# Decoder layer on one core: the first two output tiles projected together, the third as filling, and w_out's splits called later

## The chip, the core and the metric

The kernel runs on 1 core of one Trainium2 chip. The metric is the device time of one execution in microseconds (us). TensorE (PE; its weight loads PEld) does the matrix products into PSUM banks, VectorE (DVE) and ScalarE (ACT) the elementwise work, GpSimd (POOL) a little of it, and the SP queue issues the DMAs.

## The reference

One layer of a hybrid decoder, for a prompt of 2048 tokens and a sample of 8 x 8 tokens, all in float32, D_MODEL 1024:

```python
h = rms_norm(x, g_mix_pre)
proj = h @ w_in                      # q, k, v | gq, gk, gv, gr, glr
attn = swa_banded(q, k, v, sinks)    # window 128, 8 query heads on 2 key heads
log_a = log_sigmoid(glr @ w_gk2 + b_gk) / 16
o, s_new = gla_chunked(gq, gk, gv, log_a, s0)       # 4 heads, dk 64, dv 128
gla_out = rms_norm(o, g_gla) * silu(gr)
x = x + rms_norm(concat(attn, gla_out) @ w_out, g_mix_post)
u = relu(rms_norm(x, g_ffn_pre) @ w_up)
x = x + rms_norm((u * u) @ w_down, g_ffn_post)
```

The outputs are x for prompt and sample, the last 128 keys and values, and the states of the gated linear attention (GLA).

## The kernel before, in words

Tokens are cut into 17 tiles: 0 to 15 are 128 prompt tokens each, 16 (NB) is the sample. For accuracy each matrix product is made as three products of high and low parts: a tensor is "split" by a ScalarE copy that rounds (the high part) and a VectorE subtraction (the low part); `split_copy`, lines 225 and 226, is that pair.

The stages follow one another: window attention with its projections; GLA over tiles 0 to 15; the output projection with its residual and second norm; the up and down projections of the MLP. The change lies at the end of GLA and the beginning of the output projection.

GLA. `gla(i, gp, og)` is a generator that works off one tile: transposes of queries and keys (qk), decay sums (es, kd), the output gate (sg), the diagonal (pr, dg), seven levels of decayed products (`level_sums`, `leveled`: dec, XK, XQ), products of keys and queries for two levels at a time (gm), masked copies of these into AT (line 1008), the state (ds, S), the output o, its norm (ojunk, ors, og) and the output's transposes (ogT). `decayed(i)` makes the next tile's decays (pg, z, zt, tT) between the gm groups. Nearly all of this is VectorE and ScalarE work with small matmuls. To keep TensorE busy meanwhile, the generator yields numbers, and the loop that drives it then issues so many matmuls of `fill = products()`:

```python
for n, free in chain.from_iterable(parts):
    deque(islice(fill, n // 2), 0)
    for _ in range(free):
        next(side, None)
    deque(islice(fill, n - n // 2), 0)
```

For each tile the slots are 38, 14, 9, 9, 9 and 13 (`G_FILL`, `G_GM`); tile 0 has 24 instead of 38 and 20 for its own decays; the last tile has another 44 ahead of ogT. `side` is the sample's GLA.

`products()` first yields GLA's own input projection, gproj, chunk by chunk (`G_ORDER` = 3, 0, 1, 2, of 24 matmuls a tile each, the sample 16): 1408 matmuls in all. In the last tile of it, tile 15, the weights of a chunk are used for the last time, and their places take w_out: `load_wo(ks, c)` loads the pieces k of w_out (128 rows each) for the place of chunk c, over four staging places in turn (`raws[k % 4]`: two gx buffers, s0, gp_s), and splits them into `wo[k]`; its calls are spread, one for each 8 matmuls. `load_mix(i)` loads a tile's mixed features (attention and GLA outputs, transposed, from DRAM) into a place of chunk 3's weights, of which there are two in turn, and splits them. After gproj, `products()` yields the output projections (`out_projecting`) of the first two tiles of `B_ORDER` = 0, 4, 1, 5, 2, 6, 3, 7, 16, 8, 12, ..., 15: for each tile two banks, one after the other, of 8 steps k x 3 products. The lists `early` and `mixes` carry banks and features on.

What `fill` has left is issued after tile 15 (`deque(fill, 0)`). Then the loop over `B_ORDER[2:-1]` issues `out_proj(i)` for each next tile (line 1250), and `residual` for the tile two before it: squares of the banks (line 1394) and their sum (1395), the scaling by the norm (1401, which frees the banks), the addition of x (1405), the second norm (1407, 1410), transposes (xnT, 1426) and copies of these. PSUM has 8 banks: kinds a, b and c with two, d and e with one; `next_bank(kinds, ...)` goes round a string of kinds.

The instructions of an engine run in the order that is fixed when the kernel is built. `te`, `ac` and `dv` (`InOrder`) keep the order of the code; for calls through `nc.` that order can differ from the code's, as the trace shows (the first splits of w_up, called in the loop eleven tiles later, stand at 789.56 us). In the trace most calls through `te`, `ac`, `dv` and `sy` have line 139.

Of the kernel before, what the change touches and what calls it, by code (L numbers as in the profile page):

```python
# [23 lines left out]
KT = D // P  # L24
T = 2048
NB = T // P
# [35 lines left out]
G_NEXT = (NB, *range(2, NB))  # L62
G_ORDER = (3, 0, 1, 2)
G_FILL, G_GM = (38, 14, 13), 9
S_WAIT = (2, 3, 6)
WO_PARTS = ((), (0, 1, 2), (3, 4, 5), (6, 7))
B_ORDER = (*(j + b for j in range(4) for b in (0, 4)), NB, *(j + b for j in range(4) for b in (8, 12)))
# [57 lines left out]
def f32(ap):  # L125
    return ap.bitcast(F32)
# [23 lines left out]
def hybrid_step_kernel(ctx: ExitStack, tc: tile.TileContext, I, O):  # L150
    nc = tc.nc
# [11 lines left out]
    def rows(i):  # L163
        return min(P, NTOK - i * P)
# [7 lines left out]
    te, ac, dv = (InOrder(tc, engine) for engine in (nc.tensor, nc.scalar, nc.vector))  # L172
# [5 lines left out]

        return ps.tile(shape, F32, tag=kind, name=name, bufs=1 if kind in "de" else 2)

    turns = {"aabb": 0, "cdce": 0}

    def next_bank(kinds, name):
        turns[kinds] += 1
        return bank([P, 512], kinds[(turns[kinds] - 1) % len(kinds)], name)
# [37 lines left out]
    def split_copy(hi, lo, src, vector=nc.vector):  # L223

        nc.scalar.activation(hi, src, AF.Copy)
        vector.tensor_tensor(lo, src, f32(hi), op=ALU.subtract)
# [432 lines left out]
    def run(products, n=None):  # L659
        deque(products if n is None else islice(products, n), 0)  # L660
# [118 lines left out]
    for i in range(NB):  # L779
# [17 lines left out]
        if i >= NB - 2:  # L797
            t = i - NB + 2
# [100 lines left out]
    def x_place(name, shape=(P, KT, P), kind=F32R):  # L899
        return [sp.tile(list(shape), kind, tag=f"gx{u}", name=f"gx{u}_{name}", bufs=2) for u in range(2)]  # L900
# [160 lines left out]
    def gla(i, gp, og=iter(())):  # L1061
# [20 lines left out]
        for l, b in enumerate(LEVELS):  # L1082
            level_sums(before, after, dec, l, b)
            leveled(XK if l else None, XQ, dec, qk, l, b, P)
        yield G_FILL[1], 2
        following = decayed(i + 1, gps[i + 1]) if i < NB - 1 else iter(())
        nc.scalar.activation(dec[:, :, NL, :], before, AF.Exp, scale=1.0 / 16)
        qd = next(qds)
# [131 lines left out]
            te.transpose(ob[:NS, h, :], s_oT[:, h, :], ident)  # L1220
        yield from finish_out(i, lambda h: ob[:NS, h, :], sg, NS, "b")

    def load_mix(i):
        n = rows(i)
        p_, c = gw[G_ORDER[0]][0], G_ORDER[0]
        m = p_.tile([P, 3, KT, P], F32R, tag=f"w{c}{(B_ORDER.index(i) + 1) % 2}", name=f"mt_{i}")
        ks = KT // 2 if i == NB - 1 else KT
        nc.sync.dma_start(f32(m[:, 0, :ks, :n]), mix_d[i][:, :ks])
        if i == NB:
            split_copy(m[:, 1, :, :NS], m[:, 1, :, NS:], f32(m[:, 0, :, :NS]))  # L1230
            return m[:, 1], None
        split_copy(m[:, 1, :ks, :n], m[:, 2, :ks, :n], f32(m[:, 0, :ks, :n]))
        parts = [[m[:, u, k, :n] for k in range(ks)] for u in (1, 2)]
        if i == NB - 1:
            for t, late in zip(parts, late_mix):
                t.extend(late[:, h, :] for h in range(4))
        return parts

    def out_projecting(te, i, banks):
        mh, ml = mixes.pop(i, None) or load_mix(i)  # L1240
        for c in range(2):
            p_ = next_bank("aabb", f"out_{i}_{c}")
            cc = slice(c * 512, (c + 1) * 512)
            for k in range(KT):
                if i == NB:
                    products = [(mh[:, k], w) for w in wo[k]]
                else:
                    products = (mh[k], wo[k][0]), (mh[k], wo[k][1]), (ml[k], wo[k][0])
                for u, (x, w) in enumerate(products):
                    te.matmul(p_, x, w[:, cc], start=k + u == 0, stop=k == KT - 1 and u == len(products) - 1)  # L1250
                    yield
            banks.append(p_)
# [7 lines left out]
    def load_wo(ks, c):  # L1260

        parts = [gw[c][0].tile([P, 3, D], F32R, tag=f"w{c}{u}", name=f"wo{u}_{c}") for u in range(2)]
        if len(ks) == 2:
            late_mix.extend(t[:, 2, :512].rearrange("p (h t) -> p h t", h=4) for t in parts)
        for n, k in enumerate(ks):
            wo[k] = [t[:, n, :] for t in parts]
            raw = raws[k % 4]
            if k < 4:
                for r in range(2):
                    e0 = r * 256 + k * HD  # L1270
                    nc.sync.dma_start(raw[r * HD : (r + 1) * HD], w_out[e0 : e0 + HD, :])
            else:
                nc.sync.dma_start(raw, w_out[k * P : (k + 1) * P, :])
            split_copy(*wo[k], raw)
            yield

    def products():

        xT = {G_NEXT[0]: load_T(G_NEXT[0], x_first)}
        for i, after in zip(G_NEXT, (*G_NEXT[1:], None)):  # L1280
            if after is not None:
                xT[after] = load_T(after, x_place(after))
            loads = iter(())
            for c, ks in zip(G_ORDER, WO_PARTS):
                for n, _ in enumerate(projecting(i, xT[i], (c,))):
                    if n % 8 == 4:
                        next(loads, None)
                    yield
                if after is None:
                    deque(loads, 0)  # L1290
                    if not raws:
                        raws.extend(x_place("raw", (P, D), F32))
                        raws.extend((s0_place.rearrange("p b v -> p (b v)"), gp_s[:, :D]))
                    loads = load_wo(ks, c)
                    if c == G_ORDER[1]:
                        mixes.update((j, load_mix(j)) for j in B_ORDER[:2])
        deque(loads, 0)
        deque(side, 0)
        for i, after in zip(B_ORDER, B_ORDER[2:4]):
            banks = []  # L1300
            early.append((i, banks))
            yield from out_projecting(te, i, banks)
            if i == B_ORDER[0]:
                mixes[after] = load_mix(after)

    wo, pre, ogs_of, mixes, raws, late_mix = {}, {}, {}, {}, [], []
    early = []
# [62 lines left out]
    res_x = {}  # L1370
    for i in B_ORDER[:2]:
        res_x[i], loaded = load_x(i)
    with tc.issue_after(loaded.ins):
        mixes[B_ORDER[3]] = load_mix(B_ORDER[3])

    sy = InOrder(tc, nc.sync)

# [147 lines left out]
        ]  # L1525
        split_by(ac, dv, *parts, sums[g])

    for n, i in enumerate(B_ORDER[2:-1]):
        early.append((i, out_proj(i)))
        run(residual(*early.pop(0)))  # L1530
        if n == len(B_ORDER) - 5:
            load_up(0)
            split_up(0, 0, nc.scalar, nc.vector)
            split_up(0, 1, nc.scalar, nc.vector)
            (a11, a21), (a12, a22) = quarters(0)
            halves_[0, 13] = [
                U[f"s13{u}"].tile([P, KT // 2, 2, P], F32R, tag="s", name=f"s13{u}_0", bufs=1) for u in "hl"
            ]
            nc.vector.tensor_tensor(a22, a21, a22, op=ALU.add)
            nc.vector.tensor_tensor(a21, a11, a21, op=ALU.subtract)  # L1540
            for n_, src in enumerate((a22, a21)):
                split_by(nc.scalar, nc.vector, *(t[:, :, n_] for t in halves_[0, 13]), src)
            nc.vector.tensor_tensor(a22, a22, a11, op=ALU.subtract)
            nc.vector.tensor_tensor(a12, a12, a22, op=ALU.subtract)
# [493 lines left out]
```

## Time and profile before

| | us |
|---|---|
| median of 3 runs | 2285.39 (2285.17 to 2286.59) |
| the profiled execution | 2285.59 |
| its span, first to last instruction | 2283.8 |
| TensorE busy | 2208.4 (97%) |
| VectorE busy | 1622.1 (71%) |
| ScalarE busy | 1205.0 (53%) |
| mean granted TensorE clock | 0.990 |
| GLA's gproj matmuls, first to last start | 291.3 to 741.1 |
| output projection, first to last matmul start | 741.3 to 958.2 |

The times below are microseconds from the span's start. A line of the timeline gives start, busy time, engine, line of the code, operation, what is written and read, how many, and in brackets the idle time before it and what ended it. A line of the stretches gives for each engine its busy time and instructions, then the granted TensorE clock, the share of time that the DMA engines were busy, and GB/s.

### The profile page before, as it was taken

To read this page: it belongs to the slowest core of one execution; us is meant where nothing else is said; L and a number is where in the kernel's file an instruction comes from. 1 tells how busy PE (TensorE), PEld (TensorE's weight loads), DVE (VectorE), ACT (ScalarE), POOL (GpSimd) and SP (SyncE) were. 2 spreads that over 40 slices of the span, in tenths; PEclk is the share of its full clock that TensorE was granted. 3 is DMA by queue.
4 is the path that set the end of the run, shared out by engine and by line. 5 is a ranking of instruction groups with operands and counts; after the bars stand their busy time and mean duration, and the time that the engine had idled before them with its cause. 6 is when DMAs were issued, how large, how long until landed. Compare 5 with 4: busy or idle time off the path is not lost.

```text
span 2283.8 us, 34091 instructions
## 1 busy us (share of the span) xinstructions
PE 2208.4 (97%) x11800; PEld 1883.3 (82%) x11800; DVE 1622.1 (71%) x3365; ACT 1205.0 (53%) x2498; POOL 270.9 (12%) x426
## 2 busy tenths in 40 slices
PE   8999998999999899989999999999999999999997
PEld 7888887889988688868888878888888888888886
DVE  5888868888888766577767687878544545855557
ACT  5778755445555344445555565555444444544445
POOL 3566512111121110000000000000000000000000
PEclk9999999999999899999999999999999999999999
DMA  6343222121113355864554565666765755876665
GB/s 232 119 150 133 94 87 86 47 72 66 52 47 94 126 170 177 260 209 179 211 184 167 198 240 213 230 235 236 241 197 169 239 176 176 277 229 220 222 193 200
DMA packets 227346, 391.34 MB, mean 171 GB/s; under 512 B 23025, under 2 KB 135046, under 8 KB 223190
## 3 DMA queue, kind: packets, MB, share of 16 engines
q1 hardware_dynamic: 227174, 389.17, 50.7%
q8 instruction: 93, 1.52, 0.3%
q14 instruction: 79, 0.65, 0.1%
HBM read 254.56 MB, written 135.59 MB: 171 GB/s over the span
## 4 chain that ended last, share of the span: by engine, by line
PE 73%; DVE 15%; ACT 6%; issue 3%; DMA 2%; POOL 1%; DVEq 0%; SPq 0%; ACTq 0%; POOLq 0%
PE dn L139 25%; PE uc L139 7%; PE ua L139 7%; PE out L1250 7%; PE gproj L139 6%; PE ue L139 4%; PE ub L139 4%; PE ud L139 3%; DVE s L139 2%; PE proj L139 2%; DVE AT L1008 1%; PE sam L139 1%; PE dsam L139 1%; DVE XQ L987 1%; DVE pl L139 1%
## 5 line engine op out<-in xcount | busy, mean ns | idle before, releaser
L139 PE MATMUL dn<-ot,os 128*128 128x512 f32 x2688 | 622.9, 390 | 2.6 <-DVE ot L139 1.6
L139 PEld LDWEIGHTS dn<-ot,os 128*128 128x128 f32 x2688 | 503.9, 188 | 111.1 <-DVE ot L139 4.7
L139 DVE TENSOR_TENSOR os<-os 128x512 fp32r<-128x512 f32 x224 | 154.7, 690 | 229.3 <-ACT os L139 228.8
L139 ACT ACTIVATE os<-os 128x512 fp32r<-128x512 f32 x224 | 141.4, 631 | 285.3 <-DMA os<-s_d 246.1
L139 PE MATMUL gproj<-wg,gx 128*128 128x384 f32 (+1 forms) x1408 | 279.5, 348 | 1.6 <-ACT s_dec L611 1.6
L139 PEld LDWEIGHTS gproj<-wg,gx 128*128 128x128 f32 x1408 | 246.9, 191 | 12.0 <-issue 9.6
L139 ACT ACTIVATE st<-st 128x512 f32<-128x512 f32 x225 | 142.2, 632 | 140.1 <-DVE st L139 136.0
L139 PE MATMUL uc<-H,s 128*128 128x512 f32 x744 | 180.8, 392 | 4.9 <-ACT st L139 4.4
L139 PE MATMUL ua<-H,w 128*128 128x512 f32 x744 | 179.6, 390 | 0.3 <-DVE w L139 0.3
L139 PEld LDWEIGHTS uc<-H,s 128*128 128x128 f32 x744 | 140.5, 189 | 35.5 <-ACT st L139 5.2
L139 PEld LDWEIGHTS ua<-H,w 128*128 128x128 f32 x744 | 138.7, 188 | 29.3 <-DVE w L139 0.8
L215 POOL TENSOR_TENSOR frs<-rs_v,half 128x1 f32<-128x1 f32 (+1 forms) x13 | 9.2, 708 | 1261.1 <-DVE rs_v L139 1261.1
L1250 PE MATMUL out<-wo,mt 128*128 128x512 f32 x656 | 155.1, 396 | 3.2 <-DVE x L1401 3.2
L139 DVE TENSOR_TENSOR st<-st 128x512 f32<-128x512 f32 x160 | 110.4, 692 | 67.1 <-ACT st L139 63.8
L1250 PEld LDWEIGHTS out<-wo,mt 128*128 128x128 f32 x656 | 124.0, 191 | 28.9 <-DVE x L1401 3.4
L139 ACT ACTIVATE s<-t 128x1024 fp32r<-128x1024 f32 x62 | 65.8, 1061 | 59.8 <-PE ud L139 26.5
L139 DVE TENSOR_TENSOR ot<-ot 128x512 fp32r<-128x512 f32 x128 | 88.2, 689 | 12.8 <-ACT ot L139 12.1
L139 PE MATMUL proj<-wa_hi,xh 128*128 128x384 f32 (+1 forms) x272 | 95.7, 355 | 0.9 <-ACT wa_hi L139 0.6
L139 PE MATMUL proj<-wa_lo,xh 128*128 128x384 f32 (+1 forms) x272 | 94.3, 351 | 0.0
L139 PE MATMUL proj<-wa_hi,xl 128*128 128x384 f32 (+1 forms) x272 | 93.3, 347 | 0.0
L139 DVE TENSOR_TENSOR s<-t,s 128x1024 fp32r<-128x1024 f32 x62 | 76.0, 1225 | 21.4 <-ACT s L139 18.1
L139 ACT ACTIVATE ot<-ot 128x512 fp32r<-128x512 f32 x128 | 80.7, 631 | 17.7 <-DMA ot<-t_d 13.5
(403 smaller groups left out, 4092.1 us busy)
## 6 DMA issues: line engine op xcount, KB each, us to landing
os<-s_d SPq DMA_DIRECT2D x224, 256.0 KB, 2.8
s_d<-st SPq DMA_DIRECT2D x31, 1792.0 KB, 8.9
raw<-in_w_up SPq DMA_DIRECT2D x64, 512.0 KB, 7.1
ot<-t_d SPq DMA_DIRECT2D x128, 256.0 KB, 3.4
rt<-in_w_down SPq DMA_DIRECT2D x96, 256.0 KB, 3.0
t<-in_w_down SPq DMA_DIRECT2D x64, 256.0 KB, 3.6
t_d<-t SPq DMA_DIRECT2D x32, 512.0 KB, 7.9
gx<-xt_d SPq DMA_DIRECT2D x28, 512.0 KB, 4.0
```

Source lines behind the costliest of these rows:

```text
L139: ins = call(*a, **k)
L215: nc.gpsimd.tensor_tensor(out, v[:n], e, op=ALU.pow)
L987: nc.vector.tensor_tensor(xq[rr, :, l, r, : n // 2].rearrange("p g (m b) -> p g m b", b=b), dr[rr], qr[rr], op=ALU.mult)
L1008: nc.vector.copy_predicated(dst, m, gm.rearrange("p h (m b) -> p h m b", b=b))
L1250: te.matmul(p_, x, w[:, cc], start=k + u == 0, stop=k == KT - 1 and u == len(products) - 1)
```

## The change

- The first two tiles' output projections run together: the outer loop is over the steps k of w_out, and within it over the two tiles and their two banks each, so 12 matmuls for each step.
- Pieces 3 to 7 of w_out are loaded and split one for each of the steps k = 0 to 4; before, they were called in the last chunk of gproj and right behind it. Pieces 0 to 2 are called one chunk's third later.
- The splits of the first two tiles' features are called one at a time in the third chunk's projection of tile 15; before, both were called right ahead of it.
- The third tile (tile 1) is projected in `fill` too, into the two c banks. Its features are loaded at step k = 5 into gx buffers (`x_place("mt")`) and split there in place.
- The fourth tile's features (tile 5) are loaded in `products()` after the pair; before, behind the loads of x for the first residuals.
- In tile 15 the slot of 14 is 32 (`G_LAST`).
- The loop over the output projections starts at the fourth tile, with the residual of tile 0 ahead of it; the transposes of tiles 0 and 4 take the d and e banks. The turns of "aabb" start at b.

```diff
+G_LAST = 32
...
-    turns = {"aabb": 0, "cdce": 0}
+    turns = {"aabb": 2, "cdce": 0, "cc": 0}
...
-        yield G_FILL[1], 2
+        yield G_FILL[1] if i < NB - 1 else G_LAST, 2
...
-    def load_mix(i):
+    def first_mixes():
+        for i in B_ORDER[:2]:
+            mixes[i] = load_mix(i)
+            yield
+
+    def load_mix(i, lo=None, hi=None):
         n = rows(i)
+        if lo is not None:
+            nc.sync.dma_start(f32(lo), mix_d[i])
+            split_copy(hi, lo, f32(lo))
+            return [[t[:, k, :] for k in range(KT)] for t in (hi, lo)]
...
-    def out_projecting(te, i, banks):
+    def out_projecting(te, i, banks, kinds="aabb"):
...
-            p_ = next_bank("aabb", f"out_{i}_{c}")
+            p_ = next_bank(kinds, f"out_{i}_{c}")
...
-            loads = iter(())
+            loads, later = iter(()), iter(())
             for c, ks in zip(G_ORDER, WO_PARTS):
                 for n, _ in enumerate(projecting(i, xT[i], (c,))):
                     if n % 8 == 4:
                         next(loads, None)
                     yield
                 if after is None:
-                    deque(loads, 0)
-                    if not raws:
+                    if c == G_ORDER[0]:
+                        deque(loads, 0)
                         raws.extend(x_place("raw", (P, D), F32))
                         raws.extend((s0_place.rearrange("p b v -> p (b v)"), gp_s[:, :D]))
-                    loads = load_wo(ks, c)
-                    if c == G_ORDER[1]:
-                        mixes.update((j, load_mix(j)) for j in B_ORDER[:2])
+                    elif c == G_ORDER[1]:
+                        loads = chain(first_mixes(), load_wo(ks, c))
+                    else:
+                        later = chain(later, load_wo(ks, c))
         deque(loads, 0)
         deque(side, 0)
-        for i, after in zip(B_ORDER, B_ORDER[2:4]):
-            banks = []
-            early.append((i, banks))
-            yield from out_projecting(te, i, banks)
-            if i == B_ORDER[0]:
-                mixes[after] = load_mix(after)
+        pair, third = B_ORDER[:2], B_ORDER[2]
+        pairs = [(mixes.pop(i), [next_bank("aabb", f"out_{i}_{c}") for c in range(2)]) for i in pair]
+        early.extend((i, banks) for i, (_, banks) in zip(pair, pairs))
+        for k in range(KT):
+            for (mh, ml), banks in pairs:
+                if k < 5 and banks is pairs[0][1]:
+                    next(later)
+                elif k == 5 and banks is pairs[0][1]:
+                    mixes[third] = load_mix(third, *x_place("mt"))
+                for c, p_ in enumerate(banks):
+                    cc = slice(c * 512, (c + 1) * 512)
+                    for u, (x, w) in enumerate(((mh[k], wo[k][0]), (mh[k], wo[k][1]), (ml[k], wo[k][0]))):
+                        te.matmul(
+                            p_, x, w[:, cc], start=k + u == 0, stop=k == KT - 1 and u == 2, skip_group_check=True
+                        )
+                        yield
+        mixes[B_ORDER[3]] = load_mix(B_ORDER[3])
+        banks = []
+        early.append((third, banks))
+        yield from out_projecting(te, third, banks, "cc")
...
-    with tc.issue_after(loaded.ins):
-        mixes[B_ORDER[3]] = load_mix(B_ORDER[3])
...
-    for n, i in enumerate(B_ORDER[2:-1]):
+    run(residual(*early.pop(0), kinds="de"))
+    for n, i in enumerate(B_ORDER[3:-1], 1):
         early.append((i, out_proj(i)))
-        run(residual(*early.pop(0)))
+        run(residual(*early.pop(0), kinds="de" if n == 1 else None))
```

## The prediction

> **What bounds the kernel now.** I read the page first. Its engine row says that TensorE is the bound almost everywhere, so a change can only win where TensorE idles or is clocked down. I then cut the place of the change, the last gated-linear-attention tile (tile 15) and the first output projections, into stretches and asked for each engine's busy time and the granted clock.
>
> ```profile
> PE 2208.4 (97%) x11800; PEld 1883.3 (82%) x11800; DVE 1622.1 (71%) x3365; ACT 1205.0 (53%) x2498; POOL 270.9 (12%) x426
> ...
> core 0: us, PE busy (x) PEld busy (x) DVE busy (x) ACT busy (x) POOL busy (x), PEclk, DMA share, GB/s
> 722.00:737.00 15.00, 13.43 (x120) 11.43 (x119) 12.45 (x27) 11.31 (x21) 3.10 (x3) 1.00 0.36 124
> 745.50:750.00 4.50, 3.92 (x25) 2.88 (x23) 4.44 (x10) 2.96 (x7) 0.74 (x1) 1.00 0.15 58
> 750.00:755.00 5.00, 3.17 (x25) 2.24 (x25) 4.92 (x12) 1.68 (x6) 2.55 (x2) 1.00 0.00 0
> 755.00:760.00 5.00, 2.75 (x17) 1.93 (x17) 4.82 (x20) 2.25 (x7) 0.00 (x0) 1.00 0.06 9
> 760.00:763.00 3.00, 1.44 (x17) 1.35 (x18) 2.77 (x9) 0.97 (x1) 0.00 (x0) 0.68 0.40 160
> 763.00:766.70 3.70, 3.70 (x9) 2.43 (x8) 2.17 (x5) 0.09 (x1) 0.00 (x0) 0.50 0.02 4
> 779.50:782.70 3.20, 0.02 (x2) 0.02 (x1) 2.50 (x7) 0.29 (x2) 0.55 (x1) 0.82 0.49 164
> 782.70:786.00 3.30, 3.30 (x8) 2.62 (x9) 2.02 (x4) 1.43 (x3) 0.01 (x1) 0.50 0.19 77
> 786.00:789.00 3.00, 3.00 (x10) 2.33 (x9) 2.42 (x3) 0.67 (x1) 1.05 (x2) 0.60 0.94 285
> 805.00:865.00 60.00, 60.00 (x291) 50.21 (x290) 39.70 (x60) 23.95 (x50) 5.71 (x10) 1.00 0.58 189
> ```
>
> From 745.5 to 763 TensorE is idle for 0.58 + 1.83 + 2.25 + 1.56 = 6.2 us while VectorE is full, and for 3.2 us from 779.5. After each hole the clock stands at 0.50. From 805 on TensorE never idles, so what is won ahead of it should stay won. The timeline of TensorE shows who is waited for, and the chain gives the price of a tile of the output projection at full clock.
>
> ```profile
> 737.35 4.09 PE L139 MATMUL gproj<-wg,gx 128*128 128x384 f32 x22
> 741.28 3.83 PE L139 MATMUL out<-wo,mt 128*128 128x512 f32 x16
> ...
> 745.62 3.34 PE L139 MATMUL out<-wo,mt 128*128 128x512 f32 x14
> 749.46 0.45 PE L139 MATMUL gm<-XQ,qk 128*64 128x64 f32 x8 [0.50 <-DVE XQ L987]
> ...
> 756.28 2.36 PE L139 MATMUL out<-wo,mt 128*128 128x512 f32 x9
> 761.56 1.12 PE L139 MATMUL gm<-XQ,XK 128*64 128x64 f32 x16 [2.92 <-DVE AT L1008]
> 762.61 4.21 PE L139 MATMUL out<-wo,mt 128*128 128x512 f32 x9
> ...
> 768.10 3.26 PE L139 MATMUL out<-wo,mt 128*128 128x512 f32 x13
> ...
> 772.87 6.19 PE L139 MATMUL out<-wo,mt 128*128 128x512 f32 x26
> 778.90 0.60 PE L139 MATMUL ogT<-ident,og 128*128 128x128 f32 x4
> 782.68 13.84 PE L1250 MATMUL out<-wo,mt 128*128 128x512 f32 x48 [3.18 <-DVE x L1401]
> ...
> 797.39 10.90 PE out L1250 x48
> ```
>
> One output tile of 48 matmuls takes 10.90 us at full clock, 0.227 each. The third tile, at 782.68, takes 13.84: 2.9 us are clock. The 9 at 762.61 take 4.21 against 9 x 0.227 = 2.0, and with the slower gm, ds and 13 matmuls behind them I put the first clock loss at 2.8. Idle and clock together are 6.2 + 2.8 + 3.2 + 2.9 = 15.1 us, the prize of this place.
>
> Why VectorE is late, and what holds the third tile, stands in these rows of the timeline (the 4.55 and the 1.75 are pieces of the chain, SPq is the queue of the DMA issues):
>
> ```profile
> 733.06 2.36 DVE L226 TENSOR_TENSOR wo<-gx_raw,wo 128x1024 fp32r<-128x1024 f32 x2
> ...
> 739.75 4.55 DMA gp_s<-in_w_out
> ...
> 741.83 1.13 DVE L1030 SCALAR_TENSOR_TENSOR og<-o,ors,sg 128x128 f32<-128x128 f32 x4 [0.90 <-POOL ors L215]
> ...
> 745.42 1.23 DVE L226 TENSOR_TENSOR wo<-gp_s,wo 128x1024 fp32r<-128x1024 f32 x1 [0.20 <-ACT wo L225]
> 746.57 0.99 DVE L1013 SCALAR_TENSOR_TENSOR pr<-gp 128x256 f32<-128x256 f32 x1
> ...
> 760.04 4.00 DVE L1008 COPY_PREDICATED AT<-c,gm 64x128 f32<-64x128 uint8 x11
> ...
> 764.06 1.23 DVE L226 TENSOR_TENSOR mt<-mt 128x1024 fp32r<-128x1024 f32 x1
> ...
> 771.36 1.75 PE o L139 x12
> ...
> 779.10 0.33 SPq L1228 DMA_DIRECT2D mt<-mix_d  x1
> ...
> 779.54 0.69 DVE L1041 CAST wo<-ogT 128x512 fp32r<-128x512 f32 x1 [2.37 <-PE ogT L139]
> 780.87 0.15 DVE L1395 TENSOR_TENSOR ssq<-ssq 128x1 f32<-128x1 f32 x1
> ...
> 785.63 1.04 ACT L225 ACTIVATE mt<-mt 128x1024 fp32r<-128x1024 f32 x1
> 788.44 1.22 DVE L226 TENSOR_TENSOR mt<-mt 128x1024 fp32r<-128x1024 f32 x1
> ```
>
> All eight splits of w_out (733.06 the first two, 745.42 the last, 1.23 us each) run on VectorE before pr, the first work of tile 15 there; the last waits for a DMA behind a reused staging place. Only then come tile 15's seven levels, the masked copies (11 in 4.00, 0.36 each), and the gm matmuls that wait for them. At the end VectorE stands 2.37 us at L1041 for ogT, and the sums of squares that free tile 0's banks come behind it.
>
> **The change part by part.** Filling first. Up to tile 15 the slots ask for 20 + 78 + 14 x 92 = 1386 of the 1408 gproj matmuls, so 22 are left, as the x22 at 737.35 shows. Tile 15 asks for 136 before, and 22 + 96 = 118 are there, hence 26 instead of 44 in the last slot. After, it asks for 38 + 32 + 27 + 13 + 44 = 154 of 22 + 144 = 166, and 12 of the third tile come behind ogT. No matmul is added or removed: 48 move, 10.9 us of work into holes: 18 ahead of the first gm (4.1 us), 18 ahead of ogT (4.1), 12 behind it (2.7).
>
> Splits next. In the old order w_out pieces 0 to 7 are called at most one slot into tile 15. In the new one the two mixed-feature splits take two places of the third chunk, behind the decays' transposes, pieces 0 to 2 follow, and pieces 3 to 7 are called one for each step k = 0 to 4 of the pair, each 36 matmuls (8.2 us) ahead of the step that reads it. With 16 pair matmuls in the first slot, 3 and 4 are called before tile 15's levels, 5 and 6 behind them (in the slot of 32), 7 a slot later and the third tile's features at step 5. Three VectorE splits, 3.7 us, leave the front of the levels; two of them, 2.5 us, come in front of the first masked copies. Those should be done between 1.2 us (3.7 - 2.5) and 2.3 us (with two waits of VectorE there, 0.9 at og and 0.2 at the last split) earlier; I take 1.8. The DMA wait at 739.75 goes, because piece 7's place is now free long before piece 7 is called. If the splits in fact fall between the levels, VectorE has the same sum to do, and the masked copies come no earlier than the 1.2 says.
>
> Walk on from 745.6 on the old clock: 32 matmuls to 752.9, gm 0.9, 9 to 755.8, gm 0.9, 9 to 758.8; the bank of the next gm needs the first masked copies, 761.4 before and 759.6 now: 0.8 us of the 6.2 stay, 5.4 are won. Then gm, 9, gm and ds to 763.4, 13 to 766.3 (the masked copies end near 765 with piece 7 and the third tile's features between), o 1.7, 44 to 778.0, ogT 0.6, 12 to 781.3. That is where tile 1 is done; before it was 796.5. With no hole above 1 us the first 2.8 us of clock go; bounds 0 and 2.8.
>
> The fourth tile (tile 5) is what is late next. It needs tile 0's two banks, freed by two L1401 operations, and its own features, whose load is moved to the end of the pair, on the SP queue past the stores of the final state, the loads of the two norm gains and of two tiles of x. Its place is tile 4's, free at about 770, so those wait behind it till then, and behind them the L1401 of tile 0, which needs a gain; the load itself comes 9 us ahead of its old 779.10. If both are in time, nothing is lost; if the banks come as late behind ogT as before (779.5 to 782.7, 3.2), the 12 trailing matmuls cover 2.7. Bounds 0 and 3.2 of a wait, then: I take 1.2, so of the old 3.2 us 2.0 are won, and the 2.9 of clock.
>
> In tile 14 the feature splits no longer come ahead of the decays' softplus. TensorE was idle 1.6 us in 722 to 737, so 0 to 1.6 are to be had; VectorE, 12.45 of 15 us busy, sets the pace there and I take 0. Bank turns, the third tile's "cc" banks, "de" for two tiles' transposes, the third tile's features in free gx places, whose load no longer waits on SP for tile 0's: no instruction more. What hides them is TensorE's full queue from 805 on (60.00 of 60.00); a bank that came free late would cost its delay there, nothing to 3 us. I take nothing.
>
> Sum: 5.4 + 2.8 + 2.0 + 2.9 = 13.1 us. The profiled execution took 2285.59, 0.2 above the median 2285.39: 2272.5. With every term at its good end, 6.2 + 2.8 + 3.2 + 2.9 + 1.6 = 16.7: 2268.9.
>
> On the clock, the rows: two holes, of 2.92 and 3.18 us, each followed by 0.50. [...]
>
> **The rivals.** First, the hole moves to the fourth tile. Before, its features were split at 785.63 and 788.44, 10.1 us after ogT, and VectorE runs in its written order. If the split still comes that late, 10.1 - 2.7 = 7.4 us of idle and 2.9 of clock come in place of the old 6.1: the gain falls from 15.1 to 15.1 - 10.3 = 4.8, 2280.8. For it: VectorE has og, two features, L1041 and eight sums and scalings in 10 us. Against: the load starts 9 us earlier. [...]
>
> Second, VectorE stays the bound of tile 15: splits 5 and 6 fall into gaps between levels, each holding the next exponential's product by 1.2 us, the masked copies come no earlier, and TensorE waits 2.6 us at the third gm and as much again at o, with half of the clock loss back: 4.0 + 1.4 less, 2278.
>
> Third, on the other side: pieces 5, 6 and 7 come too late for steps 5, 6 and 7. TensorE is in order, and gm stands behind the pair. Each stop would be the rest of ScalarE 1.04, VectorE 1.23 and a pair of levels' masked copies 1.5 in front, 3.8 us, and up to 2.9 of clock behind each: 3 x 6.7 = 20 against a prize of 15.1, 2290. It decides from three stops of about 2.5 us each with the clock down each time. Against it: 8.2 us of matmuls, and gm besides, lie between call and use.
>
> Fourth, the filling does its work but tile 1's early end is only spent waiting for the residual of tile 0: nothing to be measured, 2283 to 2288.
>
> **How the numbers follow.** My forecast, 10 to 17 us gained, 0.60; the first rival 0.10 and the second 0.11, faster both; no change 0.08; slower 0.11. A measurement tells about 0.2%, 4.6 us. Faster 0.80 (part of the first rival ends near the bound), same 0.09, slower 0.11. The range runs from 2268.5, all terms good, to 2281.0, where the first rival ends; the likeliest case's own range is 2268.9 to 2275.6.
>
> **What would show it.** Right: 32 out matmuls in one stretch behind es with no wait at the first two gm, a wait below 1 us at the third; 44 out matmuls ahead of ogT; clock 1.00 from 745 to 800; the fourth tile starting within 2 us of the third's end, some 14 us ahead of its 797.4. Wrong: gm or out waiting for wo L226 (third rival), for AT L1008 by over 2 us (second), or the fourth tile's first matmul waiting for mt or x L1401 by over 4 us (first); or idle that comes back between 805 and 960.

## The result and the profile after

The changed kernel takes 2280.63 us (median of 11 runs, 2278.54 to 2282.54) against 2285.91 for the kernel before on the same chip (2284.91 to 2289.75): a ratio of 0.9974, interval 0.9965 to 0.9984. Measured again beside the first experiments it took 2280.14 against 2287.71, 0.9967 (0.9954 to 0.9979). It is faster by 5 to 8 us, where 13.1 were forecast. The profiled execution took 2278.73, its span is 2276.9; the one of before took 2285.59.

To see where the rest went I cut both traces at the same six events: the first output matmul, the end of the third tile (tile 1), the first up-projection matmul (ub), the first ub that reads weights of the second kind (s), the first down-projection matmul (dn), the end. The columns are the stretch, its length, then busy time and instructions of PE, PEld, DVE, ACT and POOL, the granted clock, the DMA share and GB/s. Before:

```profile
741.28:796.52 55.24, 45.84 (x229) 36.02 (x229) 38.93 (x87) 20.34 (x48) 6.96 (x9) 0.88 0.36 123
796.52:958.40 161.88, 161.88 (x777) 135.13 (x775) 102.97 (x158) 69.04 (x141) 15.44 (x28) 1.00 0.58 192
958.40:1000.25 41.85, 35.98 (x165) 28.13 (x164) 27.65 (x35) 22.73 (x36) 1.08 (x2) 0.96 0.69 233
1000.25:1628.95 628.70, 621.16 (x2862) 517.25 (x2861) 469.68 (x681) 336.90 (x510) 0.00 (x0) 1.00 0.59 211
1628.95:2283.80 654.85, 641.58 (x2817) 527.74 (x2815) 377.03 (x570) 308.91 (x516) 9.20 (x13) 0.99 0.66 211
```

The same five stretches of the changed kernel:

```profile
741.10:784.96 43.86, 41.17 (x228) 32.58 (x226) 30.63 (x75) 17.37 (x44) 5.48 (x6) 0.96 0.37 127
784.96:950.14 165.18, 163.16 (x777) 135.16 (x777) 111.00 (x170) 71.85 (x146) 17.82 (x31) 1.00 0.61 199
950.14:992.81 42.67, 37.34 (x166) 29.61 (x164) 28.47 (x36) 23.25 (x37) 1.08 (x2) 0.92 0.67 227
992.81:1621.28 628.47, 620.88 (x2863) 517.23 (x2862) 468.99 (x680) 336.44 (x509) 0.00 (x0) 1.00 0.60 211
1621.28:2276.90 655.62, 641.80 (x2817) 527.71 (x2815) 376.83 (x570) 309.12 (x516) 9.36 (x13) 0.99 0.65 211
```

The place of the change won 55.24 - 43.86 = 11.4 us between these two traces (how much of that is the clock's luck is told with the experiments). The output projections behind it, which were full of work before (161.88 of 161.88), are 3.3 us longer, 2.0 of them idle. The start of the up projection is 0.8 longer, at a clock of 0.92 instead of 0.96. The last stretch is 0.8 longer too, but that is inside its own spread (below). 11.4 - 3.3 - 0.8 - 0.8, with 0.2 from each of the two remaining places, is the 6.9 us between the two profiled executions.

TensorE's timeline in the changed kernel, in the place of the change and right behind it; what ended an idle time stands in brackets:

```profile
745.98 7.42 PE L140 MATMUL out<-wo,mt 128*128 128x512 f32 x32
753.33 0.45 PE L140 MATMUL gm<-XQ,qk 128*64 128x64 f32 x8
...
761.66 1.12 PE L140 MATMUL gm<-XQ,XK 128*64 128x64 f32 x16 [2.50 <-DVE AT L1009]
762.72 3.26 PE L140 MATMUL out<-wo,mt 128*128 128x512 f32 x9
...
773.42 8.34 PE L140 MATMUL out<-wo,gx_mt 128*128 128x512 f32 x36
781.60 0.60 PE L140 MATMUL ogT<-ident,og 128*128 128x128 f32 x4
781.95 3.02 PE L140 MATMUL out<-wo,gx_mt 128*128 128x512 f32 x12
785.46 4.80 PE L1260 MATMUL out<-wo,mt 128*128 128x512 f32 x20 [0.50 <-DVE x L1424]
790.61 1.09 PE L1449 MATMUL xnT<-ident,x 128*128 128x128 f32 x8 [0.35 <-DVE x L1433]
...
799.32 1.06 PE L1449 MATMUL xnT<-ident,x 128*128 128x128 f32 x8 [0.33 <-DVE x L1433]
...
855.05 0.73 PE L1260 MATMUL out<-wo,mt 128*128 128x512 f32 x2 [0.31 <-ACT mt L226]
856.31 10.74 PE L1260 MATMUL out<-wo,mt 128*128 128x512 f32 x46 [0.53 <-DVE mt L227]
```

The filling works: 32 matmuls behind es, no wait at the first two gm, 36 and 8 more ahead of ogT and 12 behind it; the hole of 3.18 us behind ogT has become one of 0.50, now ahead of the fourth tile. But the third gm still waits 2.50 us, and one slow window follows it (9 matmuls in 3.26 us instead of 2.0). From 785 on stand five short waits, 0.50, 0.35, 0.33, 0.31 and 0.53, together the 2.0 us: the first is what is left of the old hole, the four others are new. Part of the other 1.3 us lies around them, since the starts of two matmuls are 0.74 us apart across the wait of 0.35 where 0.23 is usual. Why the third gm is late stands in VectorE's timeline:

```profile
746.67 1.23 DVE L227 TENSOR_TENSOR wo<-gx_raw,wo 128x1024 fp32r<-128x1024 f32 x1
...
749.99 1.22 DVE L227 TENSOR_TENSOR wo<-s,wo 128x1024 fp32r<-128x1024 f32 x1
...
758.21 1.23 DVE L227 TENSOR_TENSOR wo<-gp_s,wo 128x1024 fp32r<-128x1024 f32 x1
759.36 0.42 DVE L1090 TENSOR_TENSOR qd<-qk,dec 128x256 f32<-128x256 f32 x1
759.69 1.83 DVE L1009 COPY_PREDICATED AT<-c,gm 64x128 f32<-64x128 uint8 x4
761.55 1.22 DVE L227 TENSOR_TENSOR gx_mt<-gx_mt 128x1024 fp32r<-128x1024 f32 x1
```

Three splits of w_out that were to leave the front of the masked copies are still ahead of them: two (746.67, 749.99) between the levels, one (758.21) right before. The first four copies end at 761.5, as before; VectorE does the same sum ahead of them. A wait for AT of over 2 us is what the prediction named as the sign of its second rival.

### The profile page after: what moved, and what is told of

It is laid out like the page before. It is cut to its first block, busy times and chain, and to the rows that moved or that the text cites. A ratio compares the mean times of both kernels' runs of the same rounds, so it can differ in the third digit from the quotient of the medians.

```text
span 2276.9 us, 34089 instructions
## 1 busy us (share of the span) xinstructions
PE 2206.1 (97%) x11800; PEld 1881.1 (83%) x11800; DVE 1621.0 (71%) x3365; ACT 1204.3 (53%) x2498; POOL 271.3 (12%) x426
## 4 chain that ended last, share of the span: by engine, by line
PE 70%; DVE 16%; ACT 7%; issue 3%; DMA 2%; POOL 1%; DVEq 0%; SPq 0%; ACTq 0%; POOLq 0%
PE dn L140 24%; PE ua L140 7%; PE uc L140 7%; PE gproj L140 6%; PE out L1260 4%; PE ue L140 4%; PE ub L140 4%; PE ud L140 4%; DVE s L140 2%; PE proj L140 2%; DVE AT L1009 1%; PE sam L140 1%; PE dsam L140 1%; PE out L140 1%; DVE pl L140 1%
## 5 line engine op out<-in xcount | busy, mean ns | idle before, releaser
L140 PEld LDWEIGHTS gproj<-wg,gx 128*128 128x128 f32 x1408 | 246.8, 191 | 12.2 <-issue 9.8
L1260 PE MATMUL out<-wo,mt 128*128 128x512 f32 x608 | 141.9, 392 | 1.3 <-DVE mt L227 0.5
L1260 PEld LDWEIGHTS out<-wo,mt 128*128 128x128 f32 x608 | 113.0, 188 | 25.3 <-DVE mt L227 1.0
```

The source lines that it names most:

```text
L140: ins = call(*a, **k)
```

## The experiments

Theory A: the missing gain lies in the order of VectorE's work in tile 15. Theory B: what tile 15 wins is given back behind it, in the output projections, where short waits appear. A third possibility is the granted clock, which falls to half in windows of 3.41 us (0.50 from 761.34 to 764.75 in the trace of the changed kernel).

**The same kernels again.** The changed kernel, profiled a second time:

> The changed kernel once more, on the chip of the three others, for a time and a trace beside theirs. Theory A (the gain in tile 15 is cut by VectorE's written order, and what is left passes through): 5 to 6 us under the kernel before, the third gm of tile 15 waits 2.5 us for the masked copies again, tile 1 is done about 785. Theory B (what tile 15 gains is given back behind it): the same here; both are told apart by the others.

2280.14 us (2277.3 to 2282.92, 5 runs). The stretches of its trace are 43.96, 165.40, 42.65, 628.41 and 657.58: the first four repeat within 0.2 us, the last is 2.0 longer than in the first profile of the same kernel. In front, from the first gproj to the first output matmul, it was 3.6 us shorter (445.68 against 449.33), at a clock of 1.00 where the first profile has 0.98: three stretches of 3.4 us, at 399, 423 and 457 us, are at 0.50 to 0.51 in the first and at 1.00 in the second. The stretch at 399.5 us, the first profile of this kernel:

```profile
399.50:402.90 3.40, 3.40 (x25) 3.22 (x25) 2.90 (x12) 0.69 (x3) 0.00 (x0) 0.50 0.02 7
```

and the second:

```profile
399.50:402.90 3.40, 3.40 (x41) 2.93 (x39) 3.07 (x13) 0.94 (x4) 0.00 (x0) 1.00 0.02 7
```

The same stretch of the program, at a clock of 0.50 in one execution and of 1.00 in the other: 25 matmuls and 41.

> The kernel before, profiled once more, for the spread of its stretches without any edit. If half-clock windows outside tile 15 come and go between executions, the stretches from the first gproj to the first output projection (449.8 us) and from the last output projection to the end (654.8) differ by up to 3 us from the first profile, in steps of about 1.7 with the clock; if they are fixed in the program, all stretches agree within 0.5 us.

2286.67 us. Its stretches are 55.30, 161.90, 41.90, 628.70 and 655.60 us. From the first gproj to the first output matmul it took 450.11 against 449.82, so the front agreed here within 0.3; the last stretch is 0.8 longer than in the first profile of before. So differences of a microsecond or two in the last stretch and up to 3.6 in front come without an edit, and a cause may only be read from a stretch that repeats.

**Theory A alone.** Pieces 6 and 7 and the third tile's features are called later and tied to tile 15's masked copies, so that VectorE does them afterwards:

```diff
+    masked = []
...
-        nc.vector.copy_predicated(dst, m, ...)
+        masked.append(nc.vector.copy_predicated(dst, m, ...))
...
-                if k < 5 and banks is pairs[0][1]:
-                    next(later)
-                elif k == 5 and banks is pairs[0][1]:
-                    mixes[third] = load_mix(third, *x_place("mt"))
+                if banks is pairs[0][1]:
+                    if k < 3:
+                        next(later)
+                    elif 3 < k < 6:
+                        with tc.issue_after(masked[-1].ins):
+                            next(later)
+                    elif k == 6:
+                        with tc.issue_after(masked[-1].ins):
+                            mixes[third] = load_mix(third, *x_place("mt"))
```

> Pieces 6 and 7 of w_out and the third tile's features are called later and held behind the masked copies of the first, second and third pair of levels on VectorE; nothing is added or left out. Theory A: the third gm waits under 0.5 us instead of 2.5, the clock stays at 1.00 in 755 to 770, tile 1 is done 3 to 4 us earlier (781 to 782 instead of 785), and the time is 3 to 4 us under the changed kernel. A rival inside tile 15 (VectorE's load, not its order): the wait moves to the fourth gm or to o, 2 us there, and nothing is won. Theory B: tile 1 is done earlier, but the time is within 1 us of the changed kernel.

2278.93 us (2277.16 to 2279.68), ratio 0.9959 (0.9946 to 0.9971). VectorE and TensorE in its timeline:

```profile
757.65 1.85 DVE L1011 COPY_PREDICATED AT<-c,gm 64x128 f32<-64x128 uint8 x4
759.53 1.23 DVE L229 TENSOR_TENSOR wo<-s,wo 128x1024 fp32r<-128x1024 f32 x1
...
759.64 0.69 PE L140 MATMUL gm<-XQ,XK 128*64 128x64 f32 x16 [0.82 <-DVE AT L1011]
```

and the stretch of the change, in the columns of the stretches above:

```profile
741.20:781.60 40.40, 39.55 (x227) 31.41 (x225) 30.87 (x75) 17.05 (x44) 4.98 (x6) 1.00 0.39 134
```

With the splits behind them the copies end 2 us earlier, the third gm waits 0.82 us, and the clock stays at 1.00. The stretch falls to 40.40: 14.8 us below before, of a prize put at 15.1. Theory A is shown for the place itself. But of the 3.4 us that were won there the median has only 1.2 (2280.14 to 2278.93 on the same chip, the intervals of the two ratios overlap), where 3 to 4 were expected; the stretch of the output projections is 165.90, and tile 8's features stop TensorE for 0.94 and 0.53 us (they come behind the sample tile's 32 matmuls).

**Parts of the change.** The kernel before with the third tile as filling, the slot of 32 and the new banks and turns, but with w_out's pieces called as before and no pair:

> The kernel before with the filling alone: the third tile as filling (features in gx, c banks), the slot of 32, the bank turns; the first two tiles one after the other and the pieces of w_out as before. Theory A: the pieces all stand ahead of the levels, so the masked copies come no earlier than before (761.5), the third gm waits 2.5 to 3 us, the last slot is full: tile 1 done near 785 to 786, and the time within 1 us of the changed kernel, the filling being most of the gain. Rival: pair and later pieces carry it; then the time is within 1.5 us of the kernel before.

2283.04 us (2279.72 to 2284.76), ratio 0.9980 (0.9971 to 0.9989). The third gm waits 2.95 us, gm for XQ another 0.36 and 0.77, and the first stretch is 45.70 us. Filling alone brings 9.5 of the 11.4 us of the place; the pair and the later calls, as the change has them, the other 1.9. The median is 2.9 us above the changed kernel's on the same chip, where at most 1 was expected.

The changed kernel with `G_LAST = 14` for 32:

> The changed kernel with 14 instead of 32 matmuls asked for in tile 15's slot behind the levels (the part 'more filling in the last tile' undone); the 18 go ahead of ogT, where the slot takes all that are left. The calls of the w_out pieces follow the matmuls, so the last piece's VectorE split falls behind the masked copies here, not ahead of them. If filling is what counts: TensorE reaches the gm matmuls 18 x 0.227 = 4.1 us earlier and stands there, the masked copies end at best 1.2 us earlier, so idle in 745 to 763 rises from 2.5 to about 5.4 us with one half-clock window more (1.7 us): tile 1 done 3 to 4.6 us later, time near 2284. If VectorE's order is what counts (theory A), the masked copies come 1.2 us earlier and the loss is 2.9 us at most, time near 2283. If what is won in tile 15 does not reach the end, no change: 2280 to 2281.

2283.50 us (2279.26 to 2285.72), ratio 0.9983 (0.9974 to 0.9992). TensorE and VectorE in its timeline:

```profile
761.77 1.12 PE L140 MATMUL gm<-XQ,XK 128*64 128x64 f32 x16 [5.14 <-DVE AT L1009]
...
760.25 3.99 DVE L1009 COPY_PREDICATED AT<-c,gm 64x128 f32<-64x128 uint8 x11
764.28 1.23 DVE L227 TENSOR_TENSOR wo<-gp_s,wo 128x1024 fp32r<-128x1024 f32 x1
```

and the stretch that holds the levels:

```profile
745.50:763.00 17.50, 11.99 (x92) 9.21 (x91) 16.96 (x46) 8.96 (x22) 3.76 (x3) 0.89 0.11 43
```

The last piece's split stands behind the masked copies here, and the third gm starts 19.3 us behind the first output matmul instead of 20.5: 1.2 earlier, one split. Idle in the stretch is 5.5 us (17.50 - 11.99) where 5.4 were expected, tile 1 ends 3.4 us later, and the time is about 3 above the changed kernel's on other chips. The idle time rose by 3.0 (from 2.5), which is the 4.1 us of matmuls taken out less the 1.2 of the split: here filling paid for itself one to one, and one split ahead of the copies cost its own time.

**Theory B.** The features were called one residual earlier:

```diff
         early.append((i, out_proj(i)))
+        if n < len(B_ORDER) - 4:
+            mixes[B_ORDER[n + 3]] = load_mix(B_ORDER[n + 3])
         run(residual(*early.pop(0), kinds="de" if n == 1 else None))
```

> The features of each tile from the fifth on are called one residual earlier, so that their load stands ahead of the next x row on the SP queue. Theory A says nothing on it. Theory B, in the form that the output projection's waits for features come from that queue (0.3 and 0.5 us on mt at 855, and half a us more of unhidden pipeline): those two waits go, and the time is about 1 us under the changed kernel. Rival: the x rows come later in their place, TensorE waits for xnT by as much, and the time is the same within 0.5 us.

2282.31 us (2280.53 to 2283.9), ratio 0.9973 (0.9964 to 0.9983): no gain. The waits stayed (0.47 and 0.53 us), because the SP queue kept its order: x first (850.42), then tile 8's features (851.03). In the changed kernel these rows show it (SPq is the issue of a DMA; L1433 is the second norm, L226 the split):

```profile
847.42 1.29 DVE L1433 SCALAR_TENSOR_TENSOR x<-bx,ssq,gpre 128x1024 f32<-128x1024 f32 x1 [0.72 <-POOL ssq L216]
...
848.77 0.52 SPq L1393 DMA_DIRECT2D bx<-in_x_sample  x1
849.38 0.54 SPq L1238 DMA_DIRECT2D mt<-mix_d  x1
...
853.94 1.06 ACT L226 ACTIVATE mt<-mt 128x1024 fp32r<-128x1024 f32 x1 [5.30 <-DMA mt<-mix_d]
```

The load of x waits for its place until VectorE's L1433 is done at 848.7; the load of tile 8's features stands behind it, lands at 853.9, and TensorE needs both halves from 854.7 on. So the next kernel holds the load of x back behind the features' load, on top of the VectorE order of theory A:

```diff
+        fetched.append(nc.sync.dma_start(f32(m[:, 0, :ks, :n]), mix_d[i][:, :ks]))
...
-        x = res_x.pop(i, None) or load_x(i)[0]
+        x = res_x.pop(i, None)
+        if x is None:
+            with tc.issue_after(fetched[-1].ins):
+                x = load_x(i)[0]
```

> Builds on e2_order. In the stage of the output projections every tile's load of x, which waits for a place that an L1440 of VectorE frees, is put behind the next mixed features' load on the SP queue instead of ahead of it. Theory B (part of what tile 15 wins is given back here, by loads that stand behind a waiting one): the two stops of TensorE for the sample tile's features (0.9 and 0.5 us in e2_order, 0.31 and 0.53 in the changed kernel) go, the stage's TensorE idle falls from 2.7 to about 1.3 us, and the time is 1 to 1.5 us below e2_order's 2278.9, near 2277.5. Theory A (only VectorE's order in tile 15 cost anything): no difference to e2_order within 1 us. Against both: x comes later, and the residual that adds it stops VectorE; then TensorE waits for xnT or for banks by 1 us or more and the time is e2_order's or above.

2274.71 us (2274.1 to 2275.72), ratio 0.9948 (0.9936 to 0.9961). The features that the expectation calls the sample tile's are tile 8's; their load now stands ahead of an x on the SP queue, and their split is done at 849.4, 2 us before TensorE comes to them:

```profile
842.90 0.32 SPq L1240 DMA_DIRECT2D mt<-mix_d  x1
843.32 0.38 SPq L1400 DMA_DIRECT2D bx<-in_x_prompt  x1
...
846.78 1.06 ACT L228 ACTIVATE mt<-mt 128x1024 fp32r<-128x1024 f32 x1 [1.22 <-DMA mt<-mix_d]
```

and its stretch of the output projections:

```profile
782.10:945.90 163.80, 162.63 (x777) 135.26 (x778) 111.11 (x170) 72.12 (x146) 18.36 (x31) 1.00 0.61 201
```

TensorE stops for no features any more, the stretch is 2.1 us shorter than with the VectorE order alone, idle 1.2 as expected. The time fell by 4.2 us, where 1 to 1.5 were expected: between the two profiles, 1.8 us of it lie in the up projection, where `e2_order` has two windows of half clock at 1328 us (0.50 from 1328.2 to 1335.0) and this kernel none (1.00 from 1324 to 1334), and 1.4 in the last stretch, and neither place has an edit. On another chip the same kernel:

> e6_x_behind once more, on the chip that runs e9_x_only, so that the two differ by VectorE's order in tile 15 alone. Theory A and B together: 2274 to 2276, 2.5 to 3.5 us below e9_x_only; a repeat near 2279 would say that the first 2274.7 was the clock's doing.

2275.97 us (2274.35 to 2277.31) against 2287.66, ratio 0.9950 (0.9937 to 0.9964). The first result holds; its profile has a window of half clock at 1328 us again (0.50 from 1327.80 to 1331.20), and an up projection 0.7 us longer. And the reordering of the loads without the VectorE order, and in the kernel before:

> The changed kernel with the x loads of the output projections put behind the next mixed features' load, and nothing else of e2_order: VectorE's order in tile 15 is as in the changed kernel. Theory B (3.3 us of what tile 15 wins are given back in the output projections by loads behind a waiting one): tile 1 ends as in the changed kernel, 43.8 us after the first output matmul with 2.7 us idle, the stage from there to the MLP takes 163.8 us or less instead of 165.2, and the time is 1.5 to 4 us below the changed kernel's: 2277 to 2279. If the two edits only work together (the loads matter only once tile 15 is 3.4 us earlier still): within 1 us of the changed kernel. If the half-clock windows alone made e6_x_behind fast: the stage keeps its 165.2 us.

> The kernel before with the same reordering of the x loads. The stage of the output projections had no TensorE idle there (0.00 us in 161.9), so theory B has nothing to win here: 2285 to 2288, the same as before within 1 us. If the reordering is a gain of its own that has nothing to do with the change, the time falls by 1.5 us or more; if x comes late by it, idle appears in the stage and the time rises.

The first took 2280.05 us (2279.56 to 2281.05), ratio 0.9968 (0.9955 to 0.9980); its output projections took 163.80 us instead of 165.18, as expected, but the time did not follow: it is the changed kernel's within 0.6. The 1.4 us are in the trace and not in the runs; in its trace the last stretch was 657.80 and the up projection 0.8 longer, both inside the spread of repeats. The second took 2286.44 (2284.4 to 2288.33) beside 2287.66, ratio 0.9995 (0.9987 to 1.0004): where the output projections have no idle time (161.90 of 161.90 us busy), the order of the loads was worth nothing. Its trace shows something else. Up to the end of tile 1 it runs the instructions of before, with the same idle time (9.5 us, 9.4 before), and yet the place took 52.81 us instead of 55.24:

```profile
744.30:797.11 52.81, 43.31 (x229) 34.16 (x229) 37.94 (x86) 20.36 (x48) 7.12 (x9) 0.94 0.35 118
```

The clock of the place is 0.94 here and 0.88 in both profiles of before, an estimated 3.2 us of lost clock (0.06 x 52.81) instead of 6.6 (0.12 x 55.24), so two windows of half clock instead of four; the third tile's 48 matmuls take 12.82 us instead of 13.84. So 2.4 us of the 11.4 depend on where the windows fall, and the place won 9.0 to 11.4. By the runs, partly on different chips, the two edits are worth 1.2 and 0 us alone and 4.1 to 5.4 together; by the traces 3.4 in tile 15 and 1.4 to 2.1 behind it, 4.8 to 5.5. The single parts do not agree, and that I could not settle; stretches without an edit differ by as much, so that the sums agree may be chance.

Last, the two splits of tile 15's own last features (`late_mix`), which VectorE did ahead of tile 0's sums of squares and before which it waited 1.36 us for ogT, behind tile 0's scalings:

```diff
+            def late_split():
+                nc.vector.tensor_copy(hi, pt)
+                nc.vector.tensor_tensor(lo, pt, f32(hi), op=ALU.subtract)
+            held.append(late_split)
...
-    run(residual(*early.pop(0), kinds="de"))
+    res = residual(*early.pop(0), kinds="de")
+    run(res, 2)
+    with tc.issue_after(weighted[1].ins):
+        held.pop()()
+    run(res)
```

> Builds on e6_x_behind. The two VectorE splits of tile 15's last features (L1042 and L1043 of the changed kernel, 0.69 us each) stand behind the sums of squares and the scalings of tile 0 instead of ahead of them, where VectorE waited 1.0 to 1.4 us for ogT. Theory B: the scalings begin about 2 us earlier, the stop of the fourth tile for its banks (0.50 us in the changed kernel) goes, and the stage's idle falls by about 0.5 us more; time 0.5 below e6_x_behind's, 2277. Theory A: nothing, within 0.5 us. If half-clock windows decide where the time goes, the two differ by 1.7 us or its double in either direction, at places that have none of these edits.

2276.55 us (2273.99 to 2278.2), ratio 0.9956 (0.9942 to 0.9969). The scalings moved and the fourth tile starts without a wait:

```profile
780.86 1.41 DVE L1437 SCALAR_TENSOR_TENSOR x<-out,ssq,gpost 128x512 f32<-128x512 f32 x2
782.19 0.68 DVE L1045 CAST wo<-ogT 128x512 fp32r<-128x512 f32 x1
```

and the stretch of the output projections:

```profile
783.50:946.20 162.70, 162.32 (x777) 134.99 (x776) 110.14 (x169) 72.11 (x146) 18.43 (x31) 1.00 0.61 201
```

The stretch is 162.70, within 0.8 us of before's 161.9, with 0.4 us idle. In the traces that accounts for 2.5 of the 3.3 us of the output projections: 1.4 were loads of features behind a waiting load of x, 1.1 were splits ahead of the sums that free tile 0's banks, 0.8 remain. The time did not fall; the clock is 0.92 in the next stretch (946 to 988 us) and 0.99 in the up projection, where the kernel it builds on has 0.96 and 1.00, places without an edit, and there the stretches are 0 and 1.8 us longer.

## Why the prediction was right or wrong

That it is faster was right; the forecast of 2272.5 was 8 us too low. That 2280.63 lies inside the range is luck: the range ended at 2281.0 because of the first rival, which did not come.

- Two gm without a wait, 32 matmuls in a stretch, 44 ahead of ogT and 12 behind it: as written. The hole behind ogT (2.0 taken of 3.2) and its clock loss (2.9) went altogether but for 0.50 us; the first rival, a late fourth tile, did not come, for its features were split at 776.6 and 779.6 at the latest. Not as written: tile 1 was done at 784.96 instead of 781.3, so 11.4 us were won up to there instead of 15.2.
- "What bounds": the prize of 15.1 us was right for that trace. With VectorE's order mended the place gave 14.8 against it, and 12.4 against the execution with a clock of 0.94 in the place (`e10_before_x`).
- The step that failed first is the 5.4: "the bank of the next gm needs the first masked copies, 761.4 before and 759.6 now". It took three splits away from the front of the levels and put two back, 1.2 us at the least; the third was to come a slot later. The pieces are called by count of matmuls, but on VectorE the third stands at 758.21, ahead of the copies (759.69) too. So nothing was taken off VectorE, the copies ended at 761.5 as before, the wait was 2.50 us instead of 0.8, and 1.7 was lost there. It is the second rival's 2.6 us, without its second wait at o. With the third split behind the copies (slot of 14) that gm came 1.2 us earlier, with two behind them (`e2_order`) the copies ended at 759.5 and the wait was 0.82: the 1.8 that was taken needed two splits out of the way, not one.
- With that wait the term of 2.8 us of clock fell too: one window of half clock stayed in the place (0.96 in its row), 3.41 us with 0.3 of idle in it, so worth 1.5. The wait and the window are 3.2 of the 3.7 us by which tile 1's end came later than written. For before's two holes the sum had 5.7 us of clock; its first trace has four windows of half clock there (761.08 to 767.91 and 781.56 to 788.39), at most 6.8, the execution at 0.94 an estimated two, at most 3.4.
- The larger failure is one sentence: "From 805 on TensorE never idles, so what is won ahead of it should stay won." The sum took nothing for what a late bank would cost there. That row, 60.00 of 60.00, was measured with TensorE 11 us later. VectorE and the SP queue had their work done by then because TensorE was late; with TensorE early, waits that the old time had hidden came up, and 3.3 us went back (0.5 of it is the old hole's rest, for which the sum had 1.2). The earlier tile 1 ends, counted from the first output matmul, the longer the stretch behind it: 161.9 us after 55.2, 163.7 after 47.2 (slot of 14), 164.9 after 45.7 (filling alone), 165.2 after 43.9, 165.9 after 40.4 (`e2_order`). The reordered loads take 1.4 us off it in the changed kernel and nothing in the kernel before.
- tT in tile 14: taken at 0, and so it was. The first features' ScalarE part still stands between the steps of zt, and tT waits 1.37 us; "behind the decays' transposes" is the order of the calls, not of the engine.
- Third rival, pieces late for their steps: no wait for w_out in the pair anywhere. Fourth, nothing gained but a wait for tile 0's residual: no, that wait is the 0.50.

The kernel with both edits, VectorE's order and the loads of x behind the features, is 12.2 and 11.7 us below before in its two measurements, where 13.1 were forecast for the change alone: it is faster than both kernels. Against the changed kernel's ratio of 0.9967 to 0.9974 it has 0.9948 to 0.9950.

What stays open is the last stretch (dn to the end), 654.8 to 657.9 us over all kernels, 2.0 apart in two profiles of one of them: no run here tells its cause. In the traces of before and of the changed kernel it is not the clock, which is 1.00 up to the last dn matmul (it ends at 2273.16 and 2266.32); over the whole stretch all traces have 0.99 to 1.00. TensorE waits more there, 2.6 us in before's first profile and 4.6 in the changed kernel's second. The three profiles with both edits have 656.0 to 656.1, the changed kernel's two 655.6 and 657.6.

## What to carry to other kernels

A stage without idle time (here 161.88 us busy of 161.88) has shown no slack, only that nothing was late at that time (with TensorE 11 us earlier it idled 2.0 us): before counting a gain ahead of it, ask how early its inputs (loads behind a waiting load in a queue, splits behind a waiting operation) would be if TensorE came that much earlier. Moving a call need not move the instruction (the third split stood at 758.21, ahead of the copies, all the same); look for its place on its engine, and tie it to the instruction that it has to follow. Where a kernel varies by a few microseconds, compare the same stretches of repeated traces before giving a cause to an edit.

## What the runs showed of the hardware that was not expected

In this kernel's traces the granted clock falls to half in windows of 3.41 us, one or two together: 0.50 from 761.34 to 764.75 in the changed kernel, from 761.08 to 767.91 and from 781.56 to 788.39 in the kernel before. Within each of these two traces the half-clock windows between 240 us and the last dn matmul start whole multiples of 3.41 us apart (368.81 and 399.53 nine of them, 761.08 and 781.56 six). Where this grid lies against the work differs between executions, and what a hole cost in clock differed with it. The kernel with both edits was profiled twice; in the up projection, around 1326 us, ud waits 1.88 and 0.76 us in the first, 1.87 and 0.76 in the second, with half a microsecond of work between. Three windows of the grid in each, the first profile (its half-clock window at 973.70 starts 103 windows ahead of 1325.31):

```profile
1321.90:1325.31 3.41, 2.20 (x10) 1.50 (x8) 3.01 (x5) 1.59 (x3) 0.00 (x0) 1.00 0.00 0
1325.31:1328.72 3.41, 1.98 (x7) 1.42 (x8) 2.76 (x3) 2.51 (x3) 0.00 (x0) 1.00 0.00 0
1328.72:1332.14 3.42, 3.42 (x17) 2.81 (x15) 3.35 (x6) 3.09 (x6) 0.00 (x0) 1.00 0.02 5
```

and the second:

```profile
1321.00:1324.40 3.40, 2.54 (x12) 1.77 (x10) 3.33 (x6) 1.25 (x3) 0.00 (x0) 1.00 0.00 0
1324.40:1327.80 3.40, 1.63 (x6) 1.13 (x7) 2.42 (x4) 2.86 (x4) 0.00 (x0) 1.00 0.00 0
1327.80:1331.20 3.40, 3.40 (x10) 2.63 (x9) 3.37 (x5) 2.75 (x5) 0.00 (x0) 0.50 0.02 5
```

In the first the grid cuts the hole in two, 1.21 and 1.43 us of idle, and the next window runs 17 matmuls at full clock. In the second 0.86 and 1.77 us lie in the two windows, and the next runs 10 at half. In the traces of before and of the changed kernel, between 240 us and the last dn matmul, eight windows at full clock held 1.91 to 3.41 us of idle, and each was followed by half clock. Of those with 1.5 to 1.9 us, the ones with 1.57 and 1.73 were followed by half clock and the ones with 1.51, 1.59 (in both traces), 1.64, 1.75 and 1.76 by full. In `e2_order` the wait of 0.82 us cost no clock at all (1.00 in the row of its place). Of the half-clock windows in the same two traces, those with 0.48 and 1.12 us of idle (761.08 and 781.56, behind the two holes of before) were followed by another one, and the others, with at most 0.33 us (761.34 in the changed kernel), by full clock. So each hole cost two windows in the first profile of before; `e10_before_x`, with the same idle time in the place, has 0.94 there instead of 0.88, about two fewer. Windows at 399, 423 and 457 us are at half clock in both traces behind windows with 1.15, 0.00 and 0.00 us of idle, and in the second profile of the changed kernel these stretches are at 1.00; no run here shows why.
